# One square and one sum for each load in a streaming pooling kernel

## The chip, the core and the metric

The kernel runs on one core of a Trainium2 chip. The time is that of the device, in microseconds (us). Each kernel was run several times; a median is quoted with its lowest and highest run.

Three parts of the core take part: ScalarE (ACT) squares and takes roots, VectorE (DVE) sums, and 16 DMA engines carry data between main memory and the on-chip memory. The SyncE queue (SP) issues all loads and the last stores; the ACT queue issues the other stores.

## The reference

Power-average pooling with p = 2: the root of the mean of the squares of every four neighbours.

```python
x = np.random.randn(32, 256, 4096).astype(np.float32)      # 134.22 MB
for i in range(1024):
    window = np.abs(x[:, :, 4*i : 4*i + 4]) ** 2.0
    result[:, :, i] = np.mean(window, axis=-1) ** 0.5      # 33.55 MB
```

The windows do not cross rows, so the kernel treats input and output as flat arrays and cuts them as it likes.

## The kernel before

There are three big tiles for loads ("slots") and two for results. The input is cut into 22 loads, mostly 128 partitions x 13184 columns (6.75 MB). Each load is processed in pieces; results of two loads form a group, which is stored by one transfer.

```python
    W, O_W = 13184, 6592
    X_SLOTS, O_SLOTS = 3, 2
    slots = [[(W, [4416, 4384, 4384])]] * 18
    slots += [[(6592, [3296, 3296])] * 2, [(6592, [3296, 3296]), (4216, [2112, 2104])]]
    ODD = 840                                  # a small first piece
    groups = [2] * 9 + [3, 1]                  # loads in each group of results
    late = {7, 8, 9, 10}                       # groups that the load queue stores, at the end
    in_x = {9: (2, 0), 10: (2, 4944)}          # their results lie in load tile 2
    FINE, ENDS, LAG = range(22), (), 1
    PAIRS = 16
    # ... cut ...
    for i in range(n):
        s, _, w, chunks = loads[i]
        while ahead < n and loads[ahead][0] < s + X_SLOTS:
            load(ahead)                        # waits until the slot is free
            ahead += 1
        # ... cut: choice of the result tile ...
        for step in chunks:
            v = xs[i][:, c:c + step]
            nc.scalar.activation(out=v, in_=v, func=Act.Square)
            total_sum(ots[g][:, summed:summed + step // k], v, i)
            while pending and pending[0][0] <= done - LAG:
                root(*pending.pop(0)[1:])      # root of an earlier piece; a group's last one issues its store
            # ... cut ...
            ends = summed == columns[g] // k
            if ends or i in FINE or (i in ENDS and c == w):
                pending.append((done - 1, g, ots[g][:, rooted:summed], ends))
                rooted = summed
```

`FINE` lists the loads whose every piece has a root of its own, `ENDS` those with a root at their end; any other load shares the root of its group. `total_sum` uses one reduction for loads below `PAIRS` and two pairwise sums from there on.

## Time and profile before

| | before |
|---|---|
| time, median of 3 runs | 394.73 us (394.6 to 394.79) |
| span in the profile | 392.8 us |
| bytes moved | 167.79 MB, 427 GB/s over the span |
| ACT busy, DVE busy | 292.5 us, 271.8 us |

The two rates that matter are how long a load takes from its issue to its landing, and the same for a store. These rows of the kernel before give them; the last column is the median in us:

```profile
xt<-in_x_dram SPq DMA_DIRECT2D x18, 6592.0 KB, 39.9
out_dram<-ot ACTq DMA_DIRECT2D x7, 3296.0 KB, 27.6
```

A load of 6.75 MB is moved in some 16 us when it has the DMA engines to itself (an estimate: 6.75 MB at the 432 GB/s of the middle). It takes 39.9 us from issue to landing, and the middle of the kernel has a DMA share of 1.00, so there is always work waiting, and some 24 of the 39.9 us (the rest, by that estimate) are queueing.

### The profile page before, as it was taken

How to read it: one execution, taken by the hardware profiler on the slowest of the kernel's cores; microseconds unless marked ns; L12 is line 12 of the kernel's file. 1: busy time of each engine (PE TensorE's matmuls, PEld its weight loads, DVE VectorE, ACT ScalarE, POOL GpSimd, SP SyncE). 2: the span in 40 equal slices, each digit the busy share in tenths (PEclk: the TensorE clock that was granted, in tenths of full speed). 3: DMA queues.
4: the chain of work that ended last, by engine and by line, in shares of the span. 5: the costliest groups of instructions: out<-in, count | busy, mean ns of one | idle time of the engine just before them, and what ended most of it. 6: DMA issues, size and time to landing. Idle time of an engine off the chain costs nothing.

```text
span 392.8 us, 341 instructions
## 1 busy us (share of the span) xinstructions
DVE 271.8 (69%) x77; ACT 292.5 (74%) x128; POOL 0.2 (0%) x4
## 2 busy tenths in 40 slices
DVE  1059989594959495949594959495949494778781
ACT  3088987776776777677867786868586859899990
POOL 0000000000000000000000000000000000000000
DMA  9999999999999989999999999999999999999997
GB/s 361 420 429 446 446 446 384 430 470 430 389 432 473 430 387 435 467 430 422 432 435 430 427 435 427 430 435 459 459 404 430 459 438 430 395 430 432 429 432 315
DMA packets 5024, 167.79 MB, mean 427 GB/s; under 512 B 558, under 2 KB 678, under 8 KB 926
## 3 DMA queue, kind: packets, MB, share of 16 engines
q1 hardware_dynamic: 3879, 144.04, 85.2%
q10 hardware_dynamic: 1143, 23.73, 14.0%
q14 instruction: 2, 0.02, 0.0%
HBM read 134.22 MB, written 33.55 MB: 427 GB/s over the span
## 4 chain that ended last, share of the span: by engine, by line
DMA 62%; ACT 21%; DVE 10%; issue 4%; SPq 0%; ACTq 0%
DMA xt<-in_x_dram 62%; ACT xt L143 17%; DVE ot L96 8%; ACT ot L89 3%; ACT xt L89 1%; DVE xt L105 1%; DVE xt L106 0%; ACTq L86 0%; SPq L80 0%; SPq L112 0%; ACTq L89 0%
## 5 line engine op out<-in xcount | busy, mean ns | idle before, releaser
L143 ACT ACTIVATE xt<-xt 128x4384 f32<-128x4384 f32 (+4 forms) x62 | 229.6, 3705 | 85.1 <-DMA xt<-in_x_dram 81.9
L96 DVE TENSOR_REDUCE ot<-xt 128x1096 f32<-128x4384 f32 (+1 forms) x48 | 227.0, 4731 | 90.1 <-ACT xt L143 89.8
L89 ACT ACTIVATE ot<-ot 128x1096 f32<-128x1096 f32 (+1 forms) x54 | 59.8, 1107 | 1.8 <-DVE ot L96 1.1
L105 DVE TENSOR_TENSOR xt<-xt 128x1648 f32<-128x1648 f32 (+4 forms) x14 | 28.4, 2032 | 16.0 <-ACT xt L143 16.0
L89 ACT ACTIVATE xt<-xt 128x824 f32<-128x824 f32 (+2 forms) x8 | 6.5, 817 | 1.9 <-DVE xt L106 1.9
L106 DVE TENSOR_TENSOR ot<-xt 128x1096 f32<-128x1096 f32 (+1 forms) x6 | 7.8, 1303 | 0.2
L106 DVE TENSOR_TENSOR xt<-xt 128x824 f32<-128x824 f32 (+2 forms) x8 | 7.5, 939 | 0.3
L119 DVE TENSOR_REDUCE ot<-ot 120x224 f32<-120x896 f32 x1 | 1.1, 1086 | 5.7 <-ACT ot L117 5.7
L117 ACT ACTIVATE ot<-ot 120x896 f32<-120x896 f32 x1 | 0.9, 949 | 2.7 <-DMA ot<-in_x_dram 2.7
L117 ACT ACT_TABLE_LOAD x1 | 1.3, 1283 | 0.7 <-PEq L174 0.7
L123 ACT ACT_TABLE_LOAD x1 | 1.3, 1283 | 0.0
L123 ACT ACTIVATE ot<-ot 120x224 f32<-120x224 f32 x1 | 0.4, 389 | 0.0
L174 POOL MEMSET const-bfloat16-1.0<- 128x1 bf16 x1 | 0.1, 101 | 0.0
L174 POOL MEMSET const-uint8-127<- 128x1 uint8 x1 | 0.1, 101 | 0.0
L174 POOL MEMSET const-float32-0.0<- 128x1 f32 x1 | 0.1, 99 | 0.2 <-issue 0.2
L174 POOL MEMSET const-float32-1.0<- 128x1 f32 x1 | 0.1, 99 | 0.0
## 6 DMA issues: line engine op xcount, KB each, us to landing
xt<-in_x_dram SPq DMA_DIRECT2D x18, 6592.0 KB, 39.9
out_dram<-ot ACTq DMA_DIRECT2D x7, 3296.0 KB, 27.6
xt<-in_x_dram SPq DMA_DIRECT2D x3, 3296.0 KB, 29.4
out_dram<-ot SPq DMA_DIRECT2D x2, 3296.0 KB, 30.0
out_dram<-xt SPq DMA_DIRECT2D x1, 2472.0 KB, 10.4
xt<-in_x_dram SPq DMA_DIRECT2D x1, 2108.0 KB, 26.8
out_dram<-xt SPq DMA_DIRECT2D x1, 527.0 KB, 7.1
ot<-in_x_dram SPq DMA_DIRECT2D x1, 420.0 KB, 4.0
```

What stands on the lines that cost most here:

```text
L89: nc.scalar.activation(out=o, in_=o, func=Act.Sqrt, scale=1.0 / k)
L96: nc.vector.tensor_reduce(out=o, in_=v.rearrange("p (n j) -> p n j", j=k), axis=mybir.AxisListType.X, op=add,)
L105: nc.vector.tensor_tensor(out=h, in0=q[:, :, 0:2], in1=q[:, :, 2:4], op=add)
L106: nc.vector.tensor_tensor(out=o, in0=h[:, :, 0], in1=h[:, :, 1], op=add)
L117: nc.scalar.activation(out=t, in_=t, func=Act.Square)
L119: nc.vector.tensor_reduce(out=o, in_=t.rearrange("p (n j) -> p n j", j=k), axis=mybir.AxisListType.X, op=mybir.AluOpType.add,)
L123: nc.scalar.activation(out=o, in_=o, func=Act.Sqrt, scale=1.0 / k)
L143: nc.scalar.activation(out=v, in_=v, func=Act.Square)
L174: nc = _bacc.Bacc("TRN2", target_bir_lowering=False, num_devices=1)
```

## The change

The intent is to spend fewer instructions: one square and one sum for each load, one root for each group, fewer packets for the small piece, and no waits that other waits already imply. The first three loads and the last ones stay in smaller pieces.

```diff
-    slots = [[(W, [4416, 4384, 4384])]] * 18
-    slots += [[(6592, [3296, 3296])] * 2, [(6592, [3296, 3296]), (4216, [2112, 2104])]]
+    slots = [[(W, [6592, 6592])]] * 3 + [[(W, [W])]] * 14 + [[(W, [6592, 6592])]]
+    slots += [[(6592, [6592]), (6592, [6592])], [(6592, [6592]), (4216, [2112, 2104])]]
-    FINE, ENDS, LAG = range(22), (), 1
-    PAIRS = 16
+    FINE, ENDS, LAG = {21}, {0, 19, 20}, 1
+    PAIRS = 15
 # ... cut ...
+    def follows(ins, before):
+        for b in before:
+            tc.declare_no_dep(ins.ins, b.ins, reason="follows from other waits")
 # ... cut: called for each root, sum and square, with the earlier ones that it follows anyway ...
-    Q = 120
+    Q = 30
 # ... cut ...
-    nc.scalar.activation(out=t, in_=t, func=Act.Square)
+    nc.vector.tensor_tensor(out=t, in0=t, in1=t, op=mybir.AluOpType.mult)
```

More of the change, by code (lines that the diff above doesn't have):

```diff
@@ L73 @@
     xs = {}
+    by_load = []
     def load(i):
@@ L83 @@
     ots = {}
+    stores = {}
+    by_act = []
+    sums = []
+    def follows(ins, before):
+        for b in before:
+            tc.declare_no_dep(ins.ins, b.ins, reason="follows from other waits")
     def store(g, queue):
-        queue.dma_start(out=block(of, g, k), in_=ots[g])
+        stores[g] = queue.dma_start(out=block(of, g, k), in_=ots[g])
     def root(g, o, ends):
-        nc.scalar.activation(out=o, in_=o, func=Act.Sqrt, scale=1.0 / k)
+        r = nc.scalar.activation(out=o, in_=o, func=Act.Sqrt, scale=1.0 / k)
+        follows(r, by_act[:-1] + list(stores.values()))
+        by_act.append(r)
         if ends and g not in late:
@@ L95, in total_sum @@
         if i < PAIRS:
-            nc.vector.tensor_reduce(
+            r = nc.vector.tensor_reduce(
                 out=o, in_=v.rearrange("p (n j) -> p n j", j=k),
@@ L99, in total_sum @@
             )
+            follows(r, sums[:-1])
+            sums.append(r)
             return
@@ L104, in total_sum @@
         h = front.rearrange("p (n j) -> p n j", j=2)
-        nc.vector.tensor_tensor(out=h, in0=q[:, :, 0:2], in1=q[:, :, 2:4], op=add)
-        nc.vector.tensor_tensor(out=o, in0=h[:, :, 0], in1=h[:, :, 1], op=add)
-    Q = 120
+        r = nc.vector.tensor_tensor(out=h, in0=q[:, :, 0:2], in1=q[:, :, 2:4], op=add)
+        follows(r, sums[:-1] + by_load)
+        r = nc.vector.tensor_tensor(out=o, in0=h[:, :, 0], in1=h[:, :, 1], op=add)
+        follows(r, sums[:-1])
+        sums.append(r)
+    Q = 30
     odd = ODD * P // Q
@@ L123 @@
     nc.scalar.activation(out=o, in_=o, func=Act.Sqrt, scale=1.0 / k)
-    nc.scalar.dma_start(
+    stores["odd"] = nc.scalar.dma_start(
         out=of[(total - ODD) * P // k:total * P // k].rearrange("(p w) -> p w", p=Q), in_=o,
@@ L142 @@
             v = xs[i][:, c:c + step]
-            nc.scalar.activation(out=v, in_=v, func=Act.Square)
+            r = nc.scalar.activation(out=v, in_=v, func=Act.Square)
+            follows(r, by_act[:-1])
+            by_act.append(r)
             total_sum(ots[g][:, summed:summed + step // k], v, i)
```

## The prediction

> **What bounds the kernel now.** I read the busy shares first, then the DMA rows, then the waits of the queue that issues the loads, then the timeline of the end. From the page:
>
> ```profile
> DVE 271.8 (69%) x77; ACT 292.5 (74%) x128; POOL 0.2 (0%) x4
> ...
> DMA  9999999999999989999999999999999999999997
> ...
> DMA packets 5024, 167.79 MB, mean 427 GB/s; under 512 B 558, under 2 KB 678, under 8 KB 926
> ...
> q1 hardware_dynamic: 3879, 144.04, 85.2%
> q10 hardware_dynamic: 1143, 23.73, 14.0%
> ```
>
> The two compute engines idle a quarter of the span or more. The DMA engines are busy in every slice; the shares of the two queues sum to 99.2% of 16 engines' span. The chain of waits gives 62% to the loads. So the bound is transfer: 167.79 MB, which the change does not alter. Where is the DMA not busy? Only at the ends, as the table by windows shows:
>
> ```profile
> core 0: us, DVE busy (x) ACT busy (x) POOL busy (x), PEclk, DMA share, GB/s
> 0.00:40.00 40.00, 15.27 (x5) 21.41 (x11) 0.20 (x4) 1.00 0.98 414
> ...
> 240.00:280.00 40.00, 29.23 (x8) 30.19 (x14) 0.00 (x0) 1.00 1.00 432
> ...
> 385.00:388.00 3.00, 0.00 (x0) 0.00 (x0) 0.00 (x0) 1.00 1.00 428
> 388.00:390.00 2.00, 0.00 (x0) 0.00 (x0) 0.00 (x0) 1.00 0.85 354
> 390.00:392.00 2.00, 0.00 (x0) 0.00 (x0) 0.00 (x0) 1.00 0.26 103
> ```
>
> The middle runs at 432 GB/s with share 1.00. The last compute instruction ends at 384.8 us; only stores are left, and they drain at full rate until 388. Lost time: some 2 us before the first load moves, and at the end 0.3 + 1.5 + 0.8 us of ebbing. The time of all bytes at 432 GB/s is 388.4 us, so even a perfect schedule would win under 2%.
>
> The end of the timeline shows how near compute is to mattering there:
>
> ```profile
> 342.69 16.66 SPq L86 DMA_DIRECT2D out_dram<-ot  x2
> ...
> 380.14 1.94 ACT L143 ACTIVATE xt<-xt 128x2104 f32<-128x2104 f32 x1
> 380.26 4.88 SPq L86 DMA_DIRECT2D out_dram<-xt  x2
> ```
>
> The queue of the loads carries the last four stores too (3.375, 3.375, 2.53 and 0.54 MB). Counting back from the windows: at 385.0 some 3.0 + 1.7 + 0.5 = 5.2 us of transfer are left, and the last two stores are 3.07 MB, 7.1 us at 430 GB/s. So the store ahead of them ended near 383.1, and the third store, issued at 380.26, had some 2 us to spare. That is the one thin margin of the kernel.
>
> [...]
>
> ```profile
> L96 DVE TENSOR_REDUCE ot<-xt 128x1096 f32<-128x4384 f32 x32 | 151.0, 4719 | 6.3 <-ACT xt L143 6.0
> L143 ACT ACTIVATE xt<-xt 128x4384 f32<-128x4384 f32 x36 | 138.4, 3843 | 3.3 <-ACT ot L89 3.3
> ...
> L105 DVE TENSOR_TENSOR xt<-xt 128x1648 f32<-128x1648 f32 x6 | 11.3, 1875 | 3.9 <-ACT xt L143 3.8
> ```
>
> **The change part by part.**
>
> Fewer, larger instructions. Squares go from 62 to 27, roots from 62 to 14, reductions from 48 to 18, pair sums from 28 to 18. At 94 ns of cadence for each ACT instruction that saves 83 x 0.094 = 7.8 us of ACT time; on DVE some 40 x 0.16 = 6 us, of which the small piece takes back 5.7 (its square moves there, 3584 elements instead of 896) while one load more goes over pairs (10.6 us instead of 13.9). ACT ends near 282 busy, DVE near 269. Neither is the bound: worth 0.
>
> Larger grain. Square of 13184: 11.2 us[...]. A slot comes free 25.1 us after its load lands, where three pieces needed 18.4 (110.18 to 128.51 in the chain). Three slots at some 19.6 us a load: at 25.1 us the next load has landed and the second next is on its way, not due before about 39. So the queue keeps 14 us of work when the refill is issued. Worth 0; issue to landing of a load should fall from 39.9 to some 33.
>
> Later stores. A group's root now comes as one instruction of 6592 (5.7 us) behind the next load's square: the store is issued 11.1 + 5.7 = 16.8 us after that load lands, not 4.9. It lands 27.6 us later (its row), at 44.4. The tile is written again 39.2 + 11.2 = 50.4 us after that landing. A margin of 6 us stays: worth 0. It shifts loads: the one without a store beside it should take 16 us, the next 23, instead of 19.5 each.
>
> The small piece. [...]180 fewer packets in all, none of it more than a tenth of a us. Its work now runs on DVE for 7.8 us and ends near 14, before the first load lands at 20.36. One of two table loads goes, also in idle time. Worth 0.
>
> Waits declared away. They can remove waiting instructions of some tens of ns (an event-semaphore on the load queue has a median of 17 ns). All off the path. Worth 0.
>
> The end. Here grain can cost. I chain the ACT work from the landing of load 16 (325.0): square 11.1, root of group 7 5.6 (341.7), two squares (352.8), square of load 18 (358.4), root of group 8 (364.1), squares of loads 19 and 20 (375.2), a root of 3296 (378.1), a square of 2112 (380.0). The root of load 20 waits for its pair sums: DVE starts after load 20's square at 375.3 and needs 3.6 + 1.9, so 380.8, root to 382.4: the third store is issued 2.1 us later than before. First bytes come some 0.9 us after an issue (0.73 to about 1.65 at the start), so 383.3 against the 383.1 at which the queue runs out: a gap of about 0.2 us. The last store goes out near 386.9 and the third ends near 389.3, so it adds none. Delaying store 6 lets load 16 land up to half a us earlier, which gives that back.
>
> Sum: 394.73 + 0.2, less perhaps 0.3 for lighter starts and ends: **394.6 us**.
>
> **The rivals.** (a) *The queue runs dry because slots come free late.* Each refill late by 5 us over some 18 loads would give 90 us. For it: three slots only, and 6.7 us more for each. The waits of the load queue show it waiting mostly for DVE, which looks like starvation:
>
> ```profile
> SPq L80 <- DVE ot L96: 289.4, 17, 19.0
> ```
>
> Against it: a queue that waits to issue is not an idle DMA while two loads are queued ahead, and 14 us are left. (b) *A store lands late and the DVE stalls on its output tile.* The margin is 6 us; even a stall of 5 us would fit into the 14. (c) *The tail becomes compute-bound.* If my chain is 2 us short, the store gap grows to 2 us: 396.5. (d) *Less overhead shows in full.* If ACT were the bound, 8 us would go (387); the idle 26% of ACT and the full DMA speak against it.
>
> **Range and chances.** The mechanism leaves only the tail, at most -1 us if compute there is faster and +2 if slower: 393.4 to 396.2. Faster by over 2% would need 386.8, below what the bytes take at 432 GB/s: 0.005. Slower by over 2% needs rival (a) or (b) in a form I have not seen: 0.025.
>
> **What the changed profile would show.** Right: 167.79 MB at 426 to 428 GB/s; ACT near 282 and DVE near 269 busy; 558 packets under 512 B again and about 4844 in all; load landings alternately 16 and 23 us apart; DMA digits 9 up to the last slice; the third of the last stores issued at 382 to 383. Wrong: a DMA share under 0.95 in a window of the middle (rival a or b), or full compute and a DMA gap at 383 to 386 (rival c). The prediction is wrong if the rate of the DMA depends on how loads and stores interleave, which I assume it does not.

The sum came to 394.6 us (394.73 + 0.2, less 0.3). What an instruction costs can be estimated from rows of the kernel before, and gives the numbers that the prediction counts with:

- ACT: near the end, a square of 3296 columns at 362.50, a root of 824 at 365.34 and the next square at 366.12 follow each other after 2.84 and 0.78 us. That is 0.833 ns a column and 93 ns an instruction (the prediction has 94). The busy time of one, 3843 ns for 4384 columns and 2934 for 3296, gives 11.2 us for the square of 13184.
- DVE: a reduction took 4719 ns for 4384 columns and 1086 for 896, so 1.042 ns a column and 153 ns an instruction, and 13.9 us for 13184. A pair sum took 1875 ns for 1648 columns and 1016 for 824: 1.042 ns a column and 157 ns an instruction, the 0.16 us of the prediction.

The 25.1 us for which a slot is held are the 11.2 of the square and the 13.9 of the reduction. The first bytes, which the prediction puts at about 1.65, moved in the window from 1.70 to 1.80 of the trace, 1.0 us after the issue at 0.73.

## The result, and the profile after

| | before | after |
|---|---|---|
| time, median of 6 runs each | 394.75 us (394.6 to 394.81) | 395.08 us (394.2 to 395.55) |
| span in the profile | 392.8 us | 393.3 us |

The ratio is 1.0008, with a 95% interval from 0.9995 to 1.0021: the same time.

The page of the changed kernel, in the lines that answer to those shown of before:

```profile
DVE 268.8 (68%) x38; ACT 280.7 (71%) x43; POOL 0.2 (0%) x4
...
DMA  8999999999999999999999999999999999999996
...
DMA packets 4842, 167.77 MB, mean 427 GB/s; under 512 B 558, under 2 KB 558, under 8 KB 716
...
q1 hardware_dynamic: 3789, 144.04, 85.1%
q10 hardware_dynamic: 1053, 23.73, 14.0%
...
DMA 44%; ACT 39%; DVE 14%; ACTq 0%; SPq 0%; issue 0%
...
xt<-in_x_dram SPq DMA_DIRECT2D x18, 6592.0 KB, 34.0
```

Compute became lighter: ACT has 43 instructions instead of 128 and 11.8 us less to do. The DMA rows stand still: the same 427 GB/s, the two queues again at 99.1% of the engines' span. Only the chain of waits (the row that starts with DMA 44%) has changed a lot: it gave 62% to the loads before and gives 44% now, and 39% to ACT, at the same time and the same DMA share. So that row alone does not tell what bounds this kernel. The same windows as before (window, its length, DVE, ACT and POOL busy, clock, DMA share, GB/s):

```profile
240.00:280.00 40.00, 28.17 (x3) 27.96 (x3) 0.00 (x0) 1.00 1.03 444
...
385.00:388.00 3.00, 0.93 (x2) 0.64 (x1) 0.00 (x0) 1.00 0.98 422
388.00:390.00 2.00, 0.00 (x0) 0.00 (x0) 0.00 (x0) 1.00 0.85 354
390.00:392.00 2.00, 0.00 (x0) 0.00 (x0) 0.00 (x0) 1.00 0.26 103
```

Compute now runs on past 385, but the windows of the DMA from 388 on look just as they did. Why the first line has a share over 1, 1.03, was not looked into; the line 200 to 240 has 1.00 at 431 GB/s.

What moved is inside the frame. The timeline of ACT in the middle of the changed kernel (start, length, engine, line, operation; in brackets the idle time before it and what ended it):

```profile
128.95 11.19 ACT L162 ACTIVATE xt<-xt 128x13184 f32<-128x13184 f32 x1 [8.61 <-DMA xt<-in_x_dram]
140.05 5.68 ACT L101 ACTIVATE ot<-ot 128x6592 f32<-128x6592 f32 x1
145.76 0.34 ACTq L98 DMA_DIRECT2D out_dram<-ot  x1
146.44 11.19 ACT L162 ACTIVATE xt<-xt 128x13184 f32<-128x13184 f32 x1 [0.72 <-DMA xt<-in_x_dram]
168.85 11.19 ACT L162 ACTIVATE xt<-xt 128x13184 f32<-128x13184 f32 x1 [11.22 <-DMA xt<-in_x_dram]
```

The store of a group goes out at 145.76, 16.8 us after the load at 128.95 has landed. The two intervals between squares are 17.5 and 22.4 us: in the trace the queue of the stores moved no packet from 133.1 to 149.9, so the first of the two loads had no store beside it for most of its way, and the next shared with the store issued at 145.76, whose packets ran from 149.9 to 170.7. The queue's own timeline shows that the refill of the first slot was issued at 154.09, 25.1 us after its load landed:

```profile
154.09 17.82 SPq L81 DMA_DIRECT2D xt<-in_x_dram  x2
```

At the end, the third and fourth of the last stores of the changed kernel are issued later than the 380.26 of before, the third at 382.11:

```profile
380.51 1.58 ACT L101 ACTIVATE xt<-xt 128x1648 f32<-128x1648 f32 x1 [0.78 <-DVE xt L123]
...
382.11 4.88 SPq L98 DMA_DIRECT2D out_dram<-xt  x2
```

Two questions follow. Is the time really the transfers' alone, with compute and grain worth nothing? And the changed kernel's runs scatter over 1.35 us where those of before scatter over 0.21: where does that come from, and do the 0.3 us of its median belong to it? My first theory was the last stores, which have lost their margin; the rival was the coarse middle.

### The profile page after: what moved, and what is told of

It is laid out like the page before. It is cut to its first block, busy times and chain, and to the rows that moved or that the text cites. A ratio compares the mean times of both kernels' runs of the same rounds, so it can differ in the third digit from the quotient of the medians.

```text
span 393.3 us, 193 instructions
## 1 busy us (share of the span) xinstructions
DVE 268.8 (68%) x38; ACT 280.7 (71%) x43; POOL 0.2 (0%) x4
## 2 busy tenths in 40 slices
DMA packets 4842, 167.77 MB, mean 427 GB/s; under 512 B 558, under 2 KB 558, under 8 KB 716
## 4 chain that ended last, share of the span: by engine, by line
DMA 44%; ACT 39%; DVE 14%; ACTq 0%; SPq 0%; issue 0%
DMA xt<-in_x_dram 44%; ACT xt L162 30%; DVE ot L110 12%; ACT ot L101 8%; DVE xt L121 1%; DVE xt L123 1%; ACT xt L101 1%; ACTq L98 0%; SPq L131 0%; SPq L81 0%
## 5 line engine op out<-in xcount | busy, mean ns | idle before, releaser
L162 ACT ACTIVATE xt<-xt 128x13184 f32<-128x13184 f32 (+3 forms) x27 | 222.7, 8263 | 92.3 <-DMA xt<-in_x_dram 90.6
L110 DVE TENSOR_REDUCE ot<-xt 128x3296 f32<-128x13184 f32 (+1 forms) x18 | 208.7, 11596 | 88.5 <-ACT xt L162 88.4
L101 ACT ACTIVATE ot<-ot 128x6592 f32<-128x6592 f32 (+1 forms) x10 | 51.3, 5134 | 0.0
L121 DVE TENSOR_TENSOR xt<-xt 128x3296 f32<-128x3296 f32 (+3 forms) x9 | 34.5, 3835 | 23.5 <-ACT xt L162 23.2
L123 DVE TENSOR_TENSOR ot<-xt 128x3296 f32<-128x3296 f32 (+1 forms) x4 | 10.9, 2734 | 0.1
L142 ACT ACTIVATE ot<-ot 30x896 f32<-30x896 f32 x1 | 0.9, 948 | 10.6 <-DVE ot L138 10.6
L101 ACT ACTIVATE xt<-xt 128x3296 f32<-128x3296 f32 (+3 forms) x4 | 5.8, 1449 | 2.3 <-DVE xt L123 2.3
L136 DVE TENSOR_TENSOR ot<-ot 30x3584 f32<-30x3584 f32 x1 | 3.9, 3880 | 4.8 <-DMA ot<-in_x_dram 4.8
L123 DVE TENSOR_TENSOR xt<-xt 128x1648 f32<-128x1648 f32 (+2 forms) x5 | 7.0, 1408 | 0.2
L138 DVE TENSOR_REDUCE ot<-ot 30x896 f32<-30x3584 f32 x1 | 3.9, 3875 | 0.0
L142 ACT ACT_TABLE_LOAD x1 | 1.3, 1283 | 0.7 <-PEq L195 0.7
```

What stands on the lines that cost most here:

```text
L101: r = nc.scalar.activation(out=o, in_=o, func=Act.Sqrt, scale=1.0 / k)
L110: r = nc.vector.tensor_reduce(out=o, in_=v.rearrange("p (n j) -> p n j", j=k), axis=mybir.AxisListType.X, op=add,)
L121: r = nc.vector.tensor_tensor(out=h, in0=q[:, :, 0:2], in1=q[:, :, 2:4], op=add)
L123: r = nc.vector.tensor_tensor(out=o, in0=h[:, :, 0], in1=h[:, :, 1], op=add)
L136: nc.vector.tensor_tensor(out=t, in0=t, in1=t, op=mybir.AluOpType.mult)
L138: nc.vector.tensor_reduce(out=o, in_=t.rearrange("p (n j) -> p n j", j=k), axis=mybir.AxisListType.X, op=mybir.AluOpType.add,)
```

## The experiments

Each run stands beside runs of the kernel before on the same chip; those had medians of 394.67 (first four), 394.62 (the next four), 394.54 (two slots) and 394.62 us (last two).

**1. Almost no compute.** The changed kernel, with squares, sums and roots on a few columns only; loads, stores and what they wait for remain. Its result is wrong.

```diff
+        o, v = o[:, 0:1], v[:, 0:k]                                  # in total_sum
-            r = nc.scalar.activation(out=v, in_=v, func=Act.Square)
+            r = nc.scalar.activation(out=v[:, 0:k], in_=v[:, 0:k], func=Act.Square)
-        r = nc.scalar.activation(out=o, in_=o, func=Act.Sqrt, scale=1.0 / k)
+        r = nc.scalar.activation(out=o[:, 0:1], in_=o[:, 0:1], func=Act.Sqrt, scale=1.0 / k)
+    for j in range(O_SLOTS):                                         # after the small piece
+        nc.gpsimd.memset(o_tiles[j][:, :], 1.0)
```

> The changed kernel with every square, sum and root cut down to a few columns (wrong result on purpose), all loads, stores and their order kept. Theory (transfer alone sets the time, compute touches only the last store): 393.0 to 395.0 us, ACT and DVE under 10% busy, DMA share 1.0 in the middle. Rival (the compute engines or the late release of the slots cost some of the time): below 391 us.

Measured: 394.82 us (394.79 to 395.0). Its page and one window:

```profile
DVE 13.2 (3%) x38; ACT 8.8 (2%) x43; POOL 11.4 (3%) x6
...
xt<-in_x_dram SPq DMA_DIRECT2D x18, 6592.0 KB, 56.0
```

```profile
240.00:280.00 40.00, 0.31 (x2) 0.50 (x3) 0.00 (x0) 1.00 1.00 432
```

With over 95% of the compute gone the time is that of both full kernels. This is the decisive run: neither the arithmetic nor the wait for a slot adds anything to the transfers. Slots come free at once here, so loads are issued earlier and take 56.0 us to land instead of 34.0; that figure measures how much is queued, not how fast it moves. The run has the changed kernel's number of instructions, so that their number is worth nothing rests on the change itself (205 instructions of ACT and DVE before, 81 after).

**2. A later third store.** The changed kernel with one root for loads 18 to 20 instead of two.

```diff
-    FINE, ENDS, LAG = {21}, {0, 19, 20}, 1
+    FINE, ENDS, LAG = {21}, {0}, 1
```

> The changed kernel with one root for loads 18 to 20 instead of two, so the third of the last stores goes out later by the difference of a root of 4944 and of 1648, 2.7 us: near 384.8 instead of 382.1. Theory (the queue runs out near 383 and the third store has no margin left in the changed kernel): a gap of 2 us or more in the DMA and 397.0 to 397.8 us. Rival (margin is still left, or the engines end so unevenly that a gap is absorbed): under 396.0 us.

Measured: 396.4 us (395.33 to 397.04), 1.3 us over the changed kernel's 395.08 and 1.7 over the kernel before beside it, ratio 1.0040 (1.0027 to 1.0053); between the two expectations. The store was issued at 384.49, and the gap is there in the windows of this run:

```profile
382.00:383.00 1.00, 0.02 (x1) 1.00 (x1) 0.00 (x0) 1.00 0.98 422
383.00:384.00 1.00, 0.00 (x0) 1.00 (x1) 0.00 (x0) 1.00 0.07 26
384.00:385.00 1.00, 0.00 (x0) 1.00 (x2) 0.00 (x0) 1.00 0.00 0
385.00:386.00 1.00, 0.00 (x0) 1.00 (x1) 0.00 (x0) 1.00 0.74 316
```

The DMA stands empty for 2.2 us (0.93 + 1.00 + 0.26). This profiled execution took 396.08 us, that of the changed kernel 395.09: 1.0 us more, less than the gap. The ends of the two traces, the changed kernel first, show where the rest went:

```profile
390.75:391.25 0.50, 0.00 (x0) 0.00 (x0) 0.00 (x0) 1.00 0.12 51
391.25:391.75 0.50, 0.00 (x0) 0.00 (x0) 0.00 (x0) 1.00 0.06 25
```

```profile
391.75:392.25 0.50, 0.00 (x0) 0.00 (x0) 0.00 (x0) 1.00 1.02 405
392.25:392.75 0.50, 0.00 (x0) 0.00 (x0) 0.00 (x0) 1.00 0.62 228
```

In the changed kernel the last microsecond belongs to a share of 0.12 and 0.06, one or two of the 16 engines; here the engines are full until 392.25 and done by 392.75. So nearly all bytes land some 2 us later (at 390.4 the changed kernel has 0.14 us of the 16 engines' work left, this run 2.11, summed over windows of 0.2 us), but the last packet only 1.0 us later. Why the engines finish closer together here is not shown by any run. The queue did run dry at 383, as worked out from the bytes; so the changed kernel, with its store at 382.11, sits at the edge of a real cost without paying it.

**3. The last loads in small pieces again, in the changed kernel.** Meant to restore the margin.

```diff
-    [[(W, [W])]] * 14 + [[(W, [6592, 6592])]]     # and loads 18 to 21 as before the change
+    [[(W, [W])]] * 13 + [[(W, [4416, 4384, 4384])]] * 2
-    FINE, ENDS, LAG = {21}, {0, 19, 20}, 1
+    FINE, ENDS, LAG = range(16, 22), {0}, 1
```

> The changed kernel with the pieces of the kernel before from load 16 on, so that the third store is issued near 380 again. Theory (the 0.3 us that the change lost come from the tail): 394.5 to 394.8 us and a spread of the runs as narrow as before's (0.2 us). Rival (they come from the middle, where the grain is large, or are noise): 395.0 to 395.2 us and a spread of 1 us again.

Measured: 394.96 us (394.53 to 395.53). It did not test what it should: the third store went out at 382.90, not at 380, since ACT entered the end with a root of 6592 to do and then ran more instructions without a pause: from 360 to 380 it was busy for 20.00 of 20 us with 13 instructions, in the changed kernel for 19.73 with 5. Inconclusive on the cause.

**4. The waits back.** The changed kernel with the body of `follows` emptied.

> The changed kernel without the declarations, so that all waits are back. Theory (waits that are implied cost only tens of ns off the path): within 0.3 us of the changed kernel, 394.8 to 395.4 us. Rival (they gained something that the rest of the change hid): slower than 395.7 us.

Measured: 395.26 us (395.18 to 395.67), ratio to before 1.0016 (1.0004 to 1.0029). It executes 210 instructions instead of 193. Against the changed kernel's 395.08 and, on another chip, 395.16 the declarations gain nothing that these runs can tell from zero. Two things more stand in these runs: this is the one version with the changed kernel's whole schedule whose interval excludes 1, if by a little, and its five runs lie within 0.49 us (a standard deviation of 0.20, against 0.48 for the changed kernel and 0.54 in run 8). Its grain is as coarse as the changed kernel's; what it lacks is the declarations.

**5. The small piece alone, in the kernel before.**

```diff
-    Q = 120
+    Q = 30
-    nc.scalar.activation(out=t, in_=t, func=Act.Square)
+    nc.vector.tensor_tensor(out=t, in0=t, in1=t, op=mybir.AluOpType.mult)
```

> The kernel before with the small first piece on 30 partitions and its square on VectorE, nothing else. Theory ([...]all before the first load lands): 394.5 to 394.9 us, within 0.1 us of the kernel before, spread of the runs 0.2 us. Rival (the small piece disturbs the first load and brings the spread of the changed kernel): 395.0 us or more, spread about 1 us.

What the traces show is 4842 packets in the changed kernel against 5024 before, and a small piece that landed 4.1 us after its issue against 4.0.

Measured: 394.72 us (394.62 to 395.27; four of the five within 0.24). Worth nothing, as expected; the fifth run is an outlier of a size that the kernel before shows too (395.11).

**6. The changed kernel with regrouped last loads.** The third store needs two loads instead of three.

```diff
-    groups = [2] * 9 + [3, 1]
+    groups = [2] * 9 + [2, 2]
-    in_x = {9: (2, 0), 10: (2, 4944)}
-    FINE, ENDS, LAG = {21}, {0, 19, 20}, 1
+    in_x = {9: (2, 0), 10: (2, 3296)}
+    FINE, ENDS, LAG = {21}, {0, 20}, 1
```

> The changed kernel with the last two groups of two loads each instead of three and one, so that the third of the last stores needs only loads 18 and 19 and goes out near 378, 5 us before the queue runs out; its 1.69 MB last till 387, and the last store goes out near 386.6. Theory (the third store's lost margin brings the spread and the 0.3 us): 394.5 to 394.9 us and a spread under 0.5 us. Rival (the large grain in the middle brings them): 395.0 us or more and a spread of 1 us.

Measured: 394.24 us (393.86 to 395.47). The store went out 5 us before the queue ran dry:

```profile
377.55 9.10 SPq L98 DMA_DIRECT2D out_dram<-xt  x2
```

The margin is back and the scatter, 1.61 us, has not gone. My theory of the last stores falls here.

**7. The other way round: the changed end in the kernel before.** Loads up to 15 as before, from 16 on as changed.

```diff
-    slots = [[(W, [4416, 4384, 4384])]] * 18      # and loads 18 to 21 as in the change
+    slots = [[(W, [4416, 4384, 4384])]] * 16 + [[(W, [W])], [(W, [6592, 6592])]]
-    FINE, ENDS, LAG = range(22), (), 1
+    FINE, ENDS, LAG = {*range(16), 21}, {19, 20}, 1
```

> The kernel before up to load 15 with the changed kernel's pieces from load 16 on; the third store goes out at 381 to 382. Theory (the tail brings the loss): 394.9 to 395.2 us with a spread near 1 us. Rival (the middle brings it): 394.6 to 394.8 us with a spread of 0.2 us.

Measured: 394.55 us (394.51 to 394.76), with this third store:

```profile
381.95 4.88 SPq L86 DMA_DIRECT2D out_dram<-xt  x2
```

It is issued only 0.16 us earlier than in the changed kernel, yet time and scatter are those of the kernel before. Together with run 6 this clears the end. What is left is whatever the changed kernel has and this run has not: the coarse middle (and with it one more load summed in pairs), or the declared-away waits, which no version of the kernel before carries.

**8. The changed kernel once more,** on the chip of runs 5 to 7.

> The changed kernel once more, beside the three others on this chip: 394.8 to 395.3 us with a spread of 1 us, if the spread is its own and not that of the chip of its first runs.

Measured: 395.16 us (394.25 to 395.65), ratio 1.0011 (0.9998 to 1.0023). The scatter is the kernel's own.

**9 and 10. Two load slots instead of three.** How much margin hid the coarse grain? Both kernels with the same edit; the third tile stays for the last results alone.

```diff
-    X_SLOTS, O_SLOTS = 3, 2
+    X_SLOTS, O_SLOTS = 2, 2
-    x_tiles = [... for j in range(X_SLOTS)]
+    x_tiles = [... for j in range(X_SLOTS + 1)]
```

> The changed kernel with two load slots instead of three (a third tile is kept for the last results alone). Theory (a slot is held 25.1 us after its landing,[...] and 16 us or more of transfer follow before it lands again, 43 to 51 us for two loads where the transfers need 39.2): 430 to 480 us, DMA share in the middle 0.80 to 0.92. Rival (the release time of a slot is not what the margin hangs on): under 410 us.

> The kernel before with two load slots. Theory (a slot is held 18.4 us, so 36.6 us for two loads without a store beside them, up to 42 with one, against 39.2): 397 to 425 us, well below the changed kernel with two slots, so the coarse grain's 7 us for each slot show as soon as the third slot is gone. Rival: both kernels lose alike, within 10 us of each other.

The 43 to 51 us of the first count, besides the 25.1 us of the hold and the transfer, 2.5 us for issue and landing; the 36.6 of the second, by its size, counts them too.

Measured, two runs each: the changed kernel 456.56 us (454.12 to 459.0), the kernel before 429.56 us (428.75 to 430.38). One window of each, the changed kernel first:

```profile
160.00:200.00 40.00, 27.44 (x2) 20.64 (x3) 0.00 (x0) 1.00 0.88 363
```

```profile
160.00:200.00 40.00, 25.60 (x7) 29.13 (x12) 0.00 (x0) 1.00 0.94 390
```

Without the third slot the DMA has holes in both, and the changed kernel loses 27 us more; the two differ in every part of the change, but only the grain moves the release of a slot by some 7 us (18.4 us after the landing before, 25.1 after, with three slots). The rival, that both lose alike, is out. My range for the kernel before was 5 us too low at its top: in its trace two loads take 42.5 us (squares starting at 166.13 and 208.61), which is at the top of the "36.6, up to 42" that I had worked out, in nearly every round. In the changed kernel's trace the squares on one slot start 44.8 to 47.3 us apart (148.44 to 195.77, 173.38 to 218.19), inside the 43 to 51. So the release time of a slot is a real quantity; with three slots it is worth nothing that the runs show. The 14 us of margin themselves were worked out and not measured.

**11. Late stores alone, in the kernel before.** One root for each of the groups 0 to 6.

```diff
-    FINE, ENDS, LAG = range(22), (), 1
+    FINE, ENDS, LAG = range(14, 22), (), 1
```

> The kernel before with one root a group up to group 6, so its stores go out some 10 us after the next group's first load has landed instead of 5, while slots still come free 18.4 us after a landing. Where does the spread of 1.4 us come from? Theory A (the long hold of the slots): 394.5 to 394.8 us, spread under 0.4 us. Theory B (the late stores, and the loads that land at uneven intervals): 394.9 us or more, or a spread of 1 us or more.

Measured: 394.87 us (394.81 to 395.07), ratio 1.0005 (0.9991 to 1.0019). The spread is that of theory A, the median lies between the two: 0.25 us above the kernel before beside it, nearly the 0.3 us of the change, but inside the noise. Stores went out 9.5 us after a landing (130.18 to 139.68). One premise was wrong: the big root also holds up the next pieces, so the slot of that load came free after 23.1 us (refill at 153.32), not 18.4. The run therefore shows that stores 5 us later, with every other slot held nearly as long as in the changed kernel, do not bring the scatter.

**12. The regrouped end, in the kernel before.**

```diff
-    groups = [2] * 9 + [3, 1]
-    in_x = {9: (2, 0), 10: (2, 4944)}
+    groups = [2] * 9 + [2, 2]
+    in_x = {9: (2, 0), 10: (2, 3296)}
```

> The kernel before with its last two groups of two loads each, so the third of the last stores goes out near 371 and is smaller. If an earlier and smaller third store gains by itself, as the median of the regrouped changed kernel suggested: 394.0 to 394.4 us with a spread of 0.3 us, the fastest of all. If that was the spread of the coarse middle: 394.5 to 394.8 us.

Measured: 394.59 us (394.57 to 394.64) against 394.62. The third store went out at 373.44, 7 us earlier than before, and that gains nothing. The 394.24 of run 6 was scatter. No version of the twelve beats either kernel by more than the noise.

**What stays open.** Every kernel with the coarse middle and three slots and all its work scatters by 0.5 to 1.7 us; those with the fine middle by 0.1 to 0.7, and so does the coarse one without work (0.2). The end and moderately late stores are ruled out as causes, and the small piece did not bring it (four of its five runs lie within 0.24 us). But the 0.5 of the coarse kernels is run 4, and every run with a scatter of 1 us or more has the coarse middle and the declarations together. So the cause may be the coarse middle (the full 25 us hold on both slots of a group, the stores at 16.8 us, or how loads and stores then meet), the declared-away waits, or both. Five runs are few for comparing spreads. The run that would tell, the kernel before with its implied waits declared away, was not made.

The traces show where a slower execution ends later, though not why. At 390.4 the kernel before has 0.16 us of the 16 engines' work left and the changed kernel 0.14, but the last packets land at about 391.4 and 391.8. The trace of run 8 (395.46 us) has 0.28 left at 390.4, and then a share of 0.05 to 0.06, about one engine of 16, drags on from 390.75 to 392.25. So what the changed kernel's traces show is a lag of one or two engines at the very end, not a lower rate through the middle; there is one trace of each kernel, so this is no proof for the other executions.

Nor is it shown that the median's 0.3 us are more than this scatter: the interval includes 1. Run 4's does not, at 1.0004 to 1.0029, so a loss of a few tenths of a microsecond is possible.

## Why the prediction was right

**The bound.** "So the bound is transfer": shown by run 1, where 394.82 us are left with almost nothing to compute. Of the prediction's reasons for it the DMA share of 1.00 held; the 62% of the chain was no evidence, since 44% came with the same bound.

**Fewer instructions, worth 0.** ACT ended at 280.7 us busy (said: 282), DVE at 268.8 (269). The saving is real and is spent on waiting for loads: ACT waited 90.6 us for them, 81.9 before. One term of the DVE sum is off: the small piece costs 6.7 us more on DVE (3.88 + 3.88 less 1.09), not 5.7; with 6.7 the terms give 268.8.

**Larger grain, worth 0.** The slot was held 25.1 us, as worked out. Issue to landing of a load fell from 39.9 to 34.0 us (said: some 33). The two-slot runs show, by taking the third slot away, that it is what hides the longer hold.

**Later stores, worth 0.** Issued 16.8 us after a landing, as worked out, and the intervals between squares are 17.5 and 22.4 us (said of the landings: 16 and 23). That the DMA's rate "does not" depend on how loads and stores interleave held: 427 GB/s over the span in both kernels.

**The small piece and the waits, worth 0.** Runs 5 and 4. The packets came to 4842 against "about 4844", and those under 512 B stayed at 558; of the two table loads of 1283 ns each, one is left.

**The end.** The third store was forecast for 382.4 and came at 382.11. That the queue runs out at 383.1 is confirmed by the gap in run 2. The forecast gap of about 0.2 us is not to be seen in the changed kernel's profile, nor does any run show the 0.3 us that "lighter starts and ends" were to give: these two small terms, of opposite sign, are not confirmed. A gap was counted at its full length. By the profiled pair 2.2 us of gap cost 1.0, by the medians 1.3 to 1.7, so it probably costs less, but the scatter leaves the amount open. The range, too, is not quite the sum of its words: 394.6 with -1 and +2 gives 393.6 to 396.6, not 393.4 to 396.2; the result lies in both.

**Not foreseen.** The scatter of 1.35 us. The median lies 0.5 us above 394.6; with such a scatter, agreement or difference at that level says nothing about the small terms.

## What to carry to other kernels

With the DMA share at 1.00 through the middle of this kernel, a change to the compute left two things to ask: does a buffer still come free before the queue runs out (with two slots it did not: 456.56 and 429.56 us), and is the last store still issued in time (in run 2 it was not: a gap of 2.2 us and 396.4 us)? Both margins were worked out from rows of the profile, and the run with the compute cut to a few columns measured the floor in one go (394.82 us against 395.08). The coarser grain spent margin, a hold of 25.1 us for 18.4, while the time stayed the same within the noise (395.08 us against 394.75), and taking away one buffer showed how much of it was spent (456.56 us against 429.56).
